# Columns 1024 to 1535 of gate_a on VectorE, ahead of the attention, through a ring of slab buffers

## The chip, the cores and the metric

The kernel runs on one core of a Trainium2 chip. The core has five engines that run beside each other, each through its own instructions in order: TensorE (PE in the profile, its weight loads PEld), VectorE (DVE), ScalarE (ACT), GpSimd (POOL) and SyncE (SP), which here only issues DMAs. They meet at semaphores. The metric is the time on the device in microseconds (us). Three runs of the kernel before took 1679.76, 1679.78 and 1680.25 us.

## The reference, cut to what matters

One layer: adaLN-modulated token mixing (eight mLSTM heads and a pooling mixer), then an MLP. There are 128 context tokens and 256 latent tokens, so 384 tokens in all; the context is modulated by `c_ctx`, the latents by `c`.

```python
def _adaln(cond, ada_w, ada_b):
    mod = jax.nn.silu(cond) @ ada_w + ada_b
    return mod.reshape(cond.shape[0], N_MOD, D_MODEL)      # 6 x 2048
...
    shift_a, scale_a, gate_a, shift_f, scale_f, gate_f = [mod[:, i][:, None, :] for i in range(N_MOD)]
    h = _rmsnorm(x, norm_w[0]) * (1 + scale_a) + shift_a
    proj = h @ w_in                                        # q, k, v, o, gates, u
...
    mix = jnp.concatenate([hm, hp], axis=-1) @ w_out
    x = x + gate_a * _rmsnorm(mix, norm_w[1])
    h = _rmsnorm(x, norm_w[2]) * (1 + scale_f) + shift_f
    y = jnp.square(jax.nn.relu(h @ w1)) @ w2
    x = x + gate_f * _rmsnorm(y, norm_w[3])
```

`ada_w` is 2048 x 12288 in float32, about 100 MB. The case is about the product of silu of the two condition vectors with a few of its columns: `gate_a`, modulation 2, which is first needed when the output projection `w_out` is done.

## The kernel before, in words

All large products run on TensorE as three passes each (high half by high, high by low, low by high, in a reduced float32 format), at lines 149 to 151. A weight slab of 128 x 1024 is brought in by SP (`load_w`, line 132, three raw buffers), ScalarE makes its high half (`hi`, line 138) and VectorE its low half (`lo`, line 139), four buffers each. A projection group is `gemm_T`: two accumulators of 128 x 384 and four such slabs, 24 matmuls for each. After each slab it calls its *feeds*: generators that put other work in between, so many steps for each slab as their rate says.

The stages around the change are: `u` and `v` (line 512) until about 197 us; `qk(0)`, the first group of q and k, which is eight slabs with the pooling mixer and the mLSTM gates as feeds, until about 247 us; `qk(1)` to `qk(3)`, 24 slabs with the attention of the heads before as feeds; the four groups of `o`, 16 slabs; and `w_out` (`wo`), 32 slabs, until about 610 us.

The modulation is done in two ways:

- **By TensorE** (`ada_gate`, line 239): slabs of 128 x 512 of `ada_w` are the moving operand of plain float32 matmuls with 32 columns of weights, four of them side by side in the array (a *set*). A part of 512 columns takes 16 such matmuls, four sets. Before the change, `mat` does `gate_a`'s columns 1024 to 1535 and 1536 to 2047 so, eight sets. Their slabs land in the memory of `masks` and in `gslab`. `ada_rows` then copies the sums out by ScalarE (line 277) and turns them by small matmuls (line 281).
- **By VectorE** (`ada_vec`): a slab holds two or one of the 16 rows of a partition; for each row and condition one instruction adds row times condition into the accumulator `ada_acc` (line 324 the first, `TENSOR_SCALAR`; line 326 the others, `SCALAR_TENSOR_TENSOR`). Then a set of matmuls with ones sums over the partitions (`adav`, line 339), ScalarE copies the sums out (`adav_sb`, line 341), and small matmuls turn them (`adaf`, line 345). `mid_vec` does five pieces of 1024 columns so: `scale_f`, `shift_f` and the first half of `gate_a`; as feed `ada2` it goes at 1.5 steps for each slab during `qk(1)` to `qk(3)`, then at 1.3. Its slabs are in four buffers of 512 KB of the pool `adap`. At three of its steps and at each end it moves `mat` on (`beside`).

The order within each engine is set by the Tile scheduler from the program's dependencies and its own priorities; it is fixed when the kernel is built.

Of the kernel before, what the change touches and what calls it, by code (L numbers as in the profile page):

```python
# [7 lines left out]
F32 = mybir.dt.float32  # L8
# [5 lines left out]
P = 128  # L14
# [14 lines left out]
N_ADA = 4  # L29
# [7 lines left out]
S_FIRST, S_LAST, N_LAST = 1, 6, 2  # L37
LAG = 4
N_AHEAD = 3
RATES = (1.5, 1.3, 1.3)  # L40
GATE_AT = 1, 6, 10


# [1 line left out]
def hymba_kernel(  # L45
# [6 lines left out]
    nc = tc.nc  # L52
# [6 lines left out]
    adap = ada_scope.enter_context(tc.tile_pool(name="adap", bufs=1, side="right"))  # L59
# [6 lines left out]
    def bank(name):  # L66
        return psum.tile([P, 512], F32, tag="ps", name=name)
# [11 lines left out]
    masks = vp.tile([P, N_CST - 3, P], F32, name="masks")  # L79
# [139 lines left out]
    aw = ada_w.rearrange("(p j) n -> p j n", j=16)  # L219
# [25 lines left out]
    def ada_mat(parts, tags=("ada",), raws=None):  # L245


        n, nk = len(parts), parts[0][2]
        w, nj = nk * P, 8 // nk
        ps = bank(f"ada_{parts[0][0]}_{parts[0][1]}")  # L250
        for b, (i, k0, _) in enumerate(parts):
            c0 = i * D + k0 * P
            for j0 in range(0, 16, nj):
                tag = tags[b % len(tags)]
                raw = raws.pop(0) if raws else None
                if raw is None:
                    raw = (wp if tag == "lo" else adap).tile([P, nj, w], F32, tag=tag, name=f"ada_raw_{i}_{k0}_{j0}", bufs=N_W if tag == "lo" else N_ADA)
                    nc.sync.dma_start(raw, aw[:, j0:j0 + nj, c0:c0 + w])
                for a in range(nj):
                    j = j0 + a  # L260
                    g = j % 4
                    nc.tensor.matmul(ps[32 * g:32 * g + 32, 0:w], cT[:, j, 6 - 2 * b:38 - 2 * b], raw[:, a, :],
                                     start=b == 0 and j < 4, stop=b == n - 1 and j >= 12)
                if b < n - 1 or j0 + nj < 16:
                    yield
        yield from ada_rows(parts, ps)
# [32 lines left out]
    vec = {}  # L299

    def ada_vec(i, c, n):


        acc = vec["acc"].tile([P, 2, n], F32, tag="adaacc", name=f"ada_acc_{i}_{c}", bufs=1)
        c0, nj = i * D + c, vec["slab"] // n

        def load(t):
            raw = vec["pool"].tile([P, nj, n], F32, tag="ada", name=f"ada_raw_{i}_{c}_{t}", bufs=vec["bufs"])
            nc.sync.dma_start(raw, aw[:, nj * t:nj * t + nj, c0:c0 + n])
            return raw  # L310

        beside = vec.get("beside", {})
        raw = load(0)
        yield
        for t in range(16 // nj):
            if t in beside:
                next(beside[t], None)
            more = t < 16 // nj - 1
            ahead = load(t + 1) if more and vec["bufs"] > 1 else None
            for a in range(nj):  # L320
                for g in range(2):
                    cj = sg[:, g, nj * t + a:nj * t + a + 1]
                    if t == 0 and a == 0:
                        nc.vector.tensor_scalar(acc[:, g, :], raw[:, a, :], cj, None, op0=ALU.mult)
                    else:
                        nc.vector.scalar_tensor_tensor(acc[:, g, :], raw[:, a, :], cj, acc[:, g, :], op0=ALU.mult, op1=ALU.add)  # L326
            raw = load(t + 1) if more and ahead is None else ahead
            if more:
                yield
        yield  # L330
        w = n // 2
        nk = w // P
        if "end" in beside:
            next(beside["end"], None)
        ps = bank(f"adav_{i}_{c}")
        for h in range(2):
            for g in range(2):
                r = 32 * (2 * h + g)
                nc.tensor.matmul(ps[r:r + 32, 0:w], ones[:, 0:32], acc[:, g, h * w:(h + 1) * w], start=True, stop=True)
        sb = vec["pool"].tile([P, 512], F32, tag="adasb", name=f"adav_sb_{i}_{c}", bufs=1)  # L340
        nc.scalar.activation(sb[:, 0:w], ps[:, 0:w], AF.Copy)
        yield
        pf = bank(f"adaf_{i}_{c}")
        for k in range(nk):
            nc.tensor.matmul(pf[:, 4 * k:4 + 4 * k], sb[:, k * P:(k + 1) * P], ident[:, 0:P:32], start=True, stop=True)
# [154 lines left out]
    for s in range(NS):  # L500
        for ci, (kind, c0, w) in enumerate(chunks):
            k0, nk = ksteps[s]
            load_ahead(5 * s + ci, 1 if s + ci == 0 else N_AHEAD)
            hi, lo, n = loaded.pop(5 * s + ci)
            acc = [bank(f"{kind}_{c0}_{s}_{i}") for i in range(3)]
# [295 lines left out]
        yield  # L801

    def mid_vec():
        for i, q in ((4, 0), (4, 1), (3, 0), (3, 1), (2, 0)):
            yield from ada_vec(i, 1024 * q, 1024)

    ada2 = Feed(mid_vec(), RATES[0])

    def qk(g, feeds):
        gemm_T(w_in, [g * 256], hx, NTOK, evac_q, feeds, name="q")  # L810
        gemm_T(w_in, [M + g * 256], hx, NTOK, evac_k, feeds, name="k")
# [6 lines left out]

    fxt = Feed(store_xT(), 3.0)
    fp_, fg_ = Feed(pooling(), 1.0), Feed(gates(), 1.0)  # L820
    qk(0, (fxt, fg_, fp_))
    fxt.finish()
    fg_.finish()
    fp_.finish()
# [1 line left out]
    att_scope = ExitStack()  # L826
    acc_scope = ExitStack()
    accp = acc_scope.enter_context(tc.tile_pool(name="accp", bufs=1, side="right", reuse_waits="tile"))
    vec.update(pool=adap, acc=accp, slab=1024, bufs=N_ADA)
    att = att_scope.enter_context(tc.tile_pool(name="att", bufs=2, reuse_waits="tile"))  # L830

    gslab = att.tile([P, 1, 512], F32, name="gslab", bufs=1)
    mat = ada_gate([(2, 8, 4), (2, 12, 4)], (masks.rearrange("p n q -> p (n q)").rearrange("p (j c) -> p j c", c=512), gslab))
    vec.update(beside={GATE_AT[0]: mat, GATE_AT[1]: mat, GATE_AT[2]: mat, "end": mat})
    fa = []
    for g in range(1, 4):
        fa.append(Feed(attention(g - 1), 1.0))
# [490 lines left out]
    def w1_group(g, feeds=(), n=NTOK):  # L1328
        gemm_T(w1, [grp(g)], hx2, n, evac_pair, feeds, name="w1")

    for ch in range(8):
        if ch < S_FIRST:
            w1_group(4, (ff, fx), 386)
            mlp_out(ch, (ff, fx, fn))
            fn.finish()
            for g in range(5, 8):
                w1_group(g, (ff,))
        elif ch <= S_LAST:
            if ch == S_FIRST:
                fx.finish()  # L1340
                while not vec.get("half"):
                    next(ff.gen)
                for scope in (xb_scope, acc_scope, ada_scope):
                    scope.close()
                str_scope = ExitStack()
                strp = str_scope.enter_context(tc.tile_pool(name="strp", bufs=1, side="right", reuse_waits="tile"))
                vec.update(pool=strp, acc=strp, slab=512, bufs=1, half=False)
                ff.rate = RATE_GS
                r16, r7 = strp.tile([P, 2, 2, 512], F32, name="r16"), strp.tile([P, 2, 512], F32, name="r7")
                for n in range(3):  # L1350
                    free += [wp.tile([P, 1024], F32, tag="raw", name=f"raw_a{n}", bufs=3), strp.tile([P, 1024], F32, name=f"raw_b{n}")]
# [79 lines left out]
```

## Time and profile before

| what | us |
|---|---|
| median of three runs | 1679.78 |
| the profiled execution | 1679.09 |
| its span, first to last instruction | 1677.4 |
| PE busy | 1648.3 |
| PEld busy | 1496.6 |
| DVE busy | 1328.4 |
| ACT busy | 751.1 |

The span is what the trace covers; the 1.7 us between it and the execution's time lie around it. Busy times of different engines overlap. TensorE's clock was granted in full (9 of tenths, the highest digit, in each of the 40 slices). In a timeline row the columns are the start, the length, engine, line, operation, output and inputs, shape and count; a bracket holds the idle time ahead and what ended it. In a windows row they are the stretch and its length, then the busy time of each engine with its instructions, granted clock, share of the DMA engines, and GB/s.

### The profile page before, as it was taken

Reading aid. Unit: us, or ns where it says so; the run is one execution under the profiler, and the core shown is the slowest. Engines: PE = TensorE matmul, PEld = TensorE weight load, DVE = VectorE, ACT = ScalarE, POOL = GpSimd, SP = SyncE. Lnnn points to the kernel's source line nnn. Section 1 sums busy time; section 2 is a strip of 40 time slices with the busy share of each in tenths; the row PEclk is TensorE's granted clock in tenths of the full one; section 3 lists DMA queues with packets and bytes.
Section 4 is the critical chain, followed back from the end, with each engine's and each line's share of the span. In section 5 each row is a group of like instructions: output and inputs, shape, how many; then the busy total and the mean of one; then the engine's idle time right before and its main releaser. Section 6 shows DMA issues by size and latency. Waiting matters only on the chain.

```text
span 1677.4 us, 24412 instructions
## 1 busy us (share of the span) xinstructions
PE 1648.3 (98%) x9249; PEld 1496.6 (89%) x9249; DVE 1328.4 (79%) x1971; ACT 751.1 (45%) x1224; POOL 133.1 (8%) x185
## 2 busy tenths in 40 slices
PE   6999999999999999999999999999999999999997
PEld 4888999999999989989988988988988988988986
DVE  3677669898999959997688787589788488488687
ACT  5322345555443345543444444444445354354452
POOL 1000002221000024530000000000000000000220
PEclk9999999999999999999999999999999999999999
DMA  9999757787789964754446445255544343443662
GB/s 328 329 309 304 246 175 247 239 250 229 239 262 309 319 202 137 213 153 126 136 150 203 125 133 177 87 169 162 153 151 136 116 151 116 136 125 112 197 193 103
DMA packets 231461, 320.72 MB, mean 191 GB/s; under 512 B 14784, under 2 KB 169872, under 8 KB 230960
## 3 DMA queue, kind: packets, MB, share of 16 engines
q1 hardware_dynamic: 223920, 303.42, 57.3%
q0 software_dynamic: 5984, 13.78, 2.9%
q10 hardware_dynamic: 1440, 1.97, 0.3%
q8 instruction: 72, 1.18, 0.3%
q14 instruction: 45, 0.37, 0.1%
HBM read 308.61 MB, written 10.51 MB: 190 GB/s over the span
## 4 chain that ended last, share of the span: by engine, by line
PE 78%; DVE 13%; DMA 5%; issue 3%; ACT 0%; POOL 0%; SPq 0%; DVEq 0%; ACTq 0%; POOLq 0%
PE acc_w L151 10%; PE acc_w L150 10%; PE acc_w L149 10%; PE v L512 4%; PE u L512 4%; PE y L1239 3%; PE y L1240 3%; PE y L1238 3%; DVE ada_acc L326 3%; DMA ada_raw<-in_ada_w_dram 2%; DVE lo_t L1224 2%; PE y L1082 2%; PE y L1083 2%; PE y L1081 2%; PE y_yz L1240 1%
## 5 line engine op out<-in xcount | busy, mean ns | idle before, releaser
L150 PE MATMUL acc_w<-h2l,hi_w 128*128 128x384 f32 (+1 forms) x1024 | 346.0, 338 | 0.5 <-DVE h2l L1033 0.5
L149 PE MATMUL acc_w<-h2h,hi_w 128*128 128x384 f32 (+1 forms) x1024 | 344.7, 338 | 1.2 <-ACT h2h L1029 1.2
L151 PE MATMUL acc_w<-h2h,lo_w 128*128 128x384 f32 (+1 forms) x1024 | 344.9, 337 | 0.6 <-DVE lo_w L139 0.6
L326 DVE SCALAR_TENSOR_TENSOR ada_acc<-ada_raw,sg,ada_acc 128x1024 f32<-128x1024 f32 (+1 forms) x240 | 252.8, 1081 | 32.1 <-DMA ada_raw<-in_ada_w_dram 32.1
L149 PEld LDWEIGHTS acc_w<-h2h,hi_w 128*128 128x128 f32 x1024 | 192.2, 188 | 4.0 <-ACT h2h L1029 2.0
L150 PEld LDWEIGHTS acc_w<-h2l,hi_w 128*128 128x128 f32 x1024 | 192.5, 188 | 1.8 <-DVE h2l L1033 0.8
L151 PEld LDWEIGHTS acc_w<-h2h,lo_w 128*128 128x128 f32 x1024 | 192.1, 188 | 2.2 <-DVE lo_w L139 1.9
L139 DVE TENSOR_TENSOR lo_w<-raw_b,hi_w 128x1024 fp32r<-128x1024 f32 x52 | 62.9, 1219 | 37.5 <-ACT hi_w L138 37.5
L139 DVE TENSOR_TENSOR lo_w<-raw_a,hi_w 128x1024 fp32r<-128x1024 f32 x52 | 63.1, 1219 | 35.7 <-ACT hi_w L138 35.6
L138 ACT ACTIVATE hi_w<-raw_b 128x1024 fp32r<-128x1024 f32 x52 | 54.9, 1057 | 62.7 <-PE acc_w L150 47.6
L138 ACT ACTIVATE hi_w<-raw_w 128x1024 fp32r<-128x1024 f32 x48 | 50.7, 1055 | 68.7 <-PE acc_w L150 36.5
L1223 ACT ACTIVATE hi_t<-raw_b 128x1024 fp32r<-128x1024 f32 x52 | 55.2, 1062 | 58.5 <-PE y L1240 28.3
L1223 ACT ACTIVATE hi_t<-raw_a 128x1024 fp32r<-128x1024 f32 x52 | 55.2, 1061 | 54.3 <-PE y L1240 26.5
L138 ACT ACTIVATE hi_w<-raw_a 128x1024 fp32r<-128x1024 f32 x52 | 54.8, 1057 | 53.6 <-PE acc_w L150 41.0
L139 DVE TENSOR_TENSOR lo_w<-raw_w,hi_w 128x1024 fp32r<-128x1024 f32 x48 | 58.4, 1218 | 22.0 <-ACT hi_w L138 21.9
L138 ACT ACTIVATE hi_wo<-raw_wo 128x1024 fp32r<-128x1024 f32 x32 | 33.9, 1063 | 80.1 <-DMA raw_wo<-in_w_out_dram 65.1
L1224 DVE TENSOR_TENSOR lo_b<-raw_b,hi_b 128x1024 fp32r<-128x1024 f32 x40 | 48.8, 1221 | 24.9 <-ACT hi_b L1223 24.6
L1223 ACT ACTIVATE hi_b<-raw_a 128x1024 fp32r<-128x1024 f32 x38 | 40.2, 1058 | 62.2 <-PE acc_w L150 46.2
L1223 ACT ACTIVATE hi_b<-raw_b 128x1024 fp32r<-128x1024 f32 x40 | 42.3, 1057 | 56.6 <-PE acc_w L150 45.3
L1224 DVE TENSOR_TENSOR lo_b<-raw_a,hi_b 128x1024 fp32r<-128x1024 f32 x38 | 46.2, 1221 | 22.4 <-ACT hi_b L1223 22.4
L1224 DVE TENSOR_TENSOR lo_t<-raw_a,hi_t 128x1024 fp32r<-128x1024 f32 x52 | 63.0, 1214 | 0.3 <-ACT hi_t L1223 0.2
L1224 DVE TENSOR_TENSOR lo_t<-raw_b,hi_t 128x1024 fp32r<-128x1024 f32 x52 | 62.9, 1215 | 0.0
(2286 smaller groups left out, 4243.7 us busy)
## 6 DMA issues: line engine op xcount, KB each, us to landing
ada_raw<-in_ada_w_dram SPq DMA_DIRECT2D x130, 512.0 KB, 5.2
raw_a<-in_w_dram SPq DMA_DIRECT2D x104, 512.0 KB, 4.1
raw_b<-in_w_dram SPq DMA_DIRECT2D x104, 512.0 KB, 4.2
raw_w<-in_w_dram SPq DMA_DIRECT2D x48, 512.0 KB, 4.2
raw_wo<-in_w_out_dram SPq DMA_DIRECT2D x32, 512.0 KB, 5.3
u<-in_ada_w_dram SPq DMA_DIRECT2D x18, 512.0 KB, 5.9
raw_u<-in_w_in_dram SPq DMA_DIRECT2D x16, 512.0 KB, 7.0
raw_q<-in_w_in_dram SPq DMA_DIRECT2D x16, 512.0 KB, 5.0
```

Source lines behind the costliest of these rows:

```text
L138: nc.scalar.activation(hi[:, 0:n], raw[:, 0:n], AF.Copy)
L139: low = lambda: nc.vector.tensor_tensor(lo[:, 0:n], raw[:, 0:n], hi[:, 0:n].bitcast(F32), op=ALU.subtract)
L149: nc.tensor.matmul(ps, lh, rh, start=start, stop=False)
L150: nc.tensor.matmul(ps, lh, rl, start=False, stop=False)
L151: mm3.ins = nc.tensor.matmul(ps, ll, rh, start=False, stop=stop).ins
L326: nc.vector.scalar_tensor_tensor(acc[:, g, :], raw[:, a, :], cj, acc[:, g, :], op0=ALU.mult, op1=ALU.add)
L512: nc.tensor.matmul(acc[i][:, 0:n], h[k0 + k][a][:, i * P:(i + 1) * P], (hi, lo)[b][:, k, :], start=k == 0 and a + b == 0, stop=k == nk - 1 ...
L1223: nc.scalar.activation(hi, raw, AF.Copy)
L1224: nc.vector.tensor_tensor(lo, raw, hi.bitcast(F32), op=ALU.subtract)
L1238: nc.tensor.matmul(banks[m], xh, wh, start=start and h + j == 0, stop=False)
L1239: nc.tensor.matmul(banks[m], xh, wl, start=False, stop=False)
L1240: nc.tensor.matmul(banks[m], xl, wh, start=False, stop=stop and h + j == 2)
```

## The change

Columns 1024 to 1535 of `gate_a` leave `mat` and become a first piece of `mid_vec`, 512 columns wide, with two rows in a slab. The feed `ada2` now also runs in `qk(0)`, at one step for each slab; from `qk(1)` on its rate is 1.6 instead of 1.5. The four slab buffers are now taken once, as `ring`: three hold slabs in turn, and the fourth is the accumulator of the first piece and joins the ring once its sums are taken. `mat` has one part, so four sets instead of eight, and 512 KB DMAs into the ring take the place of half of those into `masks` and `gslab`.

```diff
-RATES = (1.5, 1.3, 1.3)
+RATES = (1.6, 1.3, 1.3)
+RATE_V = 1.0
@@ ada_mat @@
+                mine = raw is None and tag == "ada" and vec.get("ring")
+                if mine:
+                    buf = mine.pop(0)
+                    raw = buf.rearrange("p (j c) -> p j c", j=nj)
+                    nc.sync.dma_start(raw, aw[:, j0:j0 + nj, c0:c0 + w])
...
+                if mine:
+                    mine.append(buf)
@@ ada_vec @@
-        acc = vec["acc"].tile([P, 2, n], F32, tag="adaacc", name=f"ada_acc_{i}_{c}", bufs=1)
+        ring, own = vec.get("ring"), vec.get("own")
+        if own is None:
+            acc = vec["acc"].tile([P, 2, n], F32, tag="adaacc", name=f"ada_acc_{i}_{c}", bufs=1)
+        else:
+            acc, vec["own"] = own.rearrange("p (g n) -> p g n", g=2), None
...
-            raw = vec["pool"].tile([P, nj, n], F32, tag="ada", name=f"ada_raw_{i}_{c}_{t}", bufs=vec["bufs"])
+            raw = (vec["pool"].tile([P, nj, n], F32, tag="ada", name=f"ada_raw_{i}_{c}_{t}", bufs=vec["bufs"]) if ring is None
+                   else ring.pop(0).rearrange("p (j c) -> p j c", j=nj))
...
+            if ring is not None:
+                ring.append(raw.rearrange("p j c -> p (j c)"))
...
+        if own is not None:
+            ring.append(own)
@@ mid_vec and its callers @@
     def mid_vec():
+        yield from ada_vec(2, 1024, 512)
+        vec.update(mid)
         for i, q in ((4, 0), (4, 1), (3, 0), (3, 1), (2, 0)):
             yield from ada_vec(i, 1024 * q, 1024)
-    ada2 = Feed(mid_vec(), RATES[0])
+    ring = [adap.tile([P, 1024], F32, tag="ada", name=f"ring{i}", bufs=N_ADA) for i in range(N_ADA)]
+    vec.update(pool=adap, slab=1024, bufs=N_ADA, ring=ring, own=ring.pop())
+    mid = {}
+    ada2 = Feed(mid_vec(), RATE_V)
...
-    qk(0, (fxt, fg_, fp_))
+    qk(0, (fxt, fg_, fp_, ada2))
...
-    vec.update(pool=adap, acc=accp, slab=1024, bufs=N_ADA)
+    vec.update(acc=accp)
+    ada2.rate = RATES[0]
...
-    mat = ada_gate([(2, 8, 4), (2, 12, 4)], (masks.rearrange("p n q -> p (n q)").rearrange("p (j c) -> p j c", c=512), gslab))
-    vec.update(beside={GATE_AT[0]: mat, GATE_AT[1]: mat, GATE_AT[2]: mat, "end": mat})
+    mat = ada_gate([(2, 12, 4)], (masks.rearrange("p n q -> p (n q)").rearrange("p (j c) -> p j c", c=512), gslab))
+    mid.update(beside={GATE_AT[0]: mat, GATE_AT[1]: mat, GATE_AT[2]: mat, "end": mat})
```

Every instruction of the five pieces that follow is placed anew with it. In the rows below, lines of the changed kernel are up to 17 higher than those before (326 is 339 now, 339 is 354, 341 is 358, 345 is 362). On VectorE, in `qk(0)` before the change, around the low halves of k's second and third slab and of the pooling mixer's third group (`p20l`, `p21l`; `lo_pw3` is from a pooling weight; `acol` to `glast` are the gates' last copies):

```order
L645 COPY acol_2056<-ps_col_2329 128x3x8 x2
L645 COPY ecol_2057<-ps_col_2335 128x24 x2
L645 COPY gcol_2058<-ps_col_2341 128x2x8 x2
L649 COPY nT_2060<-ps_n0_2346 128x16
L650 COPY glast_2059<-ps_n0_2346 128x40
L139 TENSOR_TENSOR lo_k_1024_1_2433<-raw_k_1024_1_2430,hi_k_1024_1_2432 128x1024
L139 TENSOR_TENSOR lo_k_1024_2_2482<-raw_k_1024_2_2479,hi_k_1024_2_2481 128x1024
L139 TENSOR_TENSOR lo_pw3_2528<-raw_pw3_2525,hi_pw3_2527 128x512
L200 TENSOR_TENSOR p20l_2413<-pool_2_0_2408,p20h_2412 128x384
L200 TENSOR_TENSOR p21l_2421<-pool_2_1_2416,p21h_2420 128x384
```

and with it (`ring0` to `ring2` are slabs, `ring3` is the accumulator):

```order
L667 COPY glast_2059<-ps_n0_2361 128x40
L140 TENSOR_TENSOR lo_k_1024_1_2458<-raw_k_1024_1_2455,hi_k_1024_1_2457 128x1024
L339 SCALAR_TENSOR_TENSOR ring3_2069<-ring2_2068,sg_111,ring3_2069 128x512 x2
L140 TENSOR_TENSOR lo_k_1024_2_2512<-raw_k_1024_2_2509,hi_k_1024_2_2511 128x1024
L339 SCALAR_TENSOR_TENSOR ring3_2069<-ring2_2068,sg_111,ring3_2069 128x512 x2
L339 SCALAR_TENSOR_TENSOR ring3_2069<-ring0_2066,sg_111,ring3_2069 128x512 x2
L140 TENSOR_TENSOR lo_pw3_2558<-raw_pw3_2555,hi_pw3_2557 128x512
L201 TENSOR_TENSOR p20l_2433<-pool_2_0_2428,p20h_2432 128x384
L201 TENSOR_TENSOR p21l_2441<-pool_2_1_2436,p21h_2440 128x384
L339 SCALAR_TENSOR_TENSOR ring3_2069<-ring0_2066,sg_111,ring3_2069 128x512 x2
L339 SCALAR_TENSOR_TENSOR ring3_2069<-ring1_2067,sg_111,ring3_2069 128x512 x4
```

Of the 32 new instructions, 26 now stand ahead of `p20l_2433`, six behind `p21l_2441`, and none behind k's last low half.

On TensorE, at the end of the first piece of 1024 columns (`adav_0`, `adaf_0`; `num` and `inter` are the attention's), in `qk(2)`'s k, before the change:

```order
L749 MATMUL inter_1_0_3410<-C_1_0_3136,q_2855 128x129
L749 MATMUL inter_1_0_3410<-C_1_2_1_3325,q_2855 128x129
L742 MATMUL num_1_1_3424<-v_84,e_3135 128x129 x2
L749 MATMUL inter_1_1_3427<-C_1_0_3136,q_2857 128x129
L749 MATMUL inter_1_1_3427<-C_1_2_1_3325,q_2857 128x129
L345 MATMUL adaf_0_3444<-cst,adav_sb_0_3368 128x4 x4
L149 MATMUL acc_k_0_3374<-hh_739,hi_k_1_3455 128x384
```

There `adav_0` stands 31 rows ahead of `adaf_0`, behind the set of `ada_gate` that precedes k's first slab: a whole slab and the attention's eight matmuls lie between the two. With the change:

```order
L766 MATMUL inter_2_1_3526<-C_1_1_0_3355,q_2900 128x129
L766 MATMUL inter_2_1_3526<-C_1_1_3174,q_2900 128x129
L240 MATMUL ada_gate<-masks,cT 32x512 x3
L240 MATMUL ada_gate<-gslab,cT 32x512
L354 MATMUL adav_0_3547<-ada_acc_0_2805,cst 32x512 x4
L150 MATMUL acc_k_0_3403<-hh_1187,hi_k_2_3565 128x384
L151 MATMUL acc_k_0_3403<-hl_1188,hi_k_2_3565 128x384
L152 MATMUL acc_k_0_3403<-hh_1187,lo_k_2_3566 128x384
L150 MATMUL acc_k_1_3404<-hh_1187,hi_k_2_3565 128x384
L151 MATMUL acc_k_1_3404<-hl_1188,hi_k_2_3565 128x384
L362 MATMUL adaf_0_3554<-cst,adav_sb_0_3552 128x4 x4
L152 MATMUL acc_k_1_3404<-hh_1187,lo_k_2_3566 128x384
```

The set and `adav_0` have moved to the next slab but one, and five matmuls of `acc_k` are left between `adav_0` and `adaf_0`. At two other ends of pieces it is alike: six matmuls between the pair `adav_1024` and `adaf_1024` of the second piece (24 slab matmuls and more before), and four at the end of the last piece (24 before). The new first piece has nine between its pair.

On ScalarE, around the copy `adav_sb_0` that stands between the two, before the change:

```order
L138 ACTIVATE hi_k_3_3566<-raw_k_3_3564 128x1024
L755 ACTIVATE dn_0_0_3336<-num_0_0_3332 128x2
L755 ACTIVATE dn_0_1_3347<-num_0_1_3343 128x2
L758 ACTIVATE hs_0_3331<-num_0_0_3332,dn_0_0_3336 128x128
L758 ACTIVATE hs_0_3331<-num_0_1_3343,dn_0_1_3347 128x128
L341 ACTIVATE adav_sb_0_3368<-adav_0_3363 128x512
L760 ACTIVATE sq_0_3335,ssh<-hs_0_3331 128x128
L760 ACTIVATE sq_1_3346,ssh<-hs_0_3331 128x128
L138 ACTIVATE hi_q_0_3610<-raw_q_0_3608 128x1024
```

and with it:

```order
L139 ACTIVATE hi_q_1_3723<-raw_q_1_3721 128x1024
L768 ACTIVATE nsb_2_0_3510<-inter_2_0_3509,gcol 128x129 x2
L768 ACTIVATE nsb_2_1_3527<-inter_2_1_3526,gcol 128x129 x2
L772 ACTIVATE dn_2_0_3516<-nsb_2_0_3510 128x2
L772 ACTIVATE dn_2_1_3533<-nsb_2_1_3527 128x2
L775 ACTIVATE hs_2_3505<-nsb_2_0_3510,dn_2_0_3516 128x128
L775 ACTIVATE hs_2_3505<-nsb_2_1_3527,dn_2_1_3533 128x128
L358 ACTIVATE adav_sb_0_3552<-adav_0_3547 128x512
L777 ACTIVATE nsb_2_0_3510,ssh<-hs_2_3505 128x128
L777 ACTIVATE nsb_2_1_3527,ssh<-hs_2_3505 128x128
```

The copy has moved from behind `hs_0`, the first outputs' scaling, to behind both scalings of `hs_2`, the third outputs' (each waits for `dn_2`, which VectorE makes from `nsb_2`, and that from `inter_2`).

More of the change, by code (lines that the diff above doesn't have):

```diff
@@ L255, in ada_mat @@
                 raw = raws.pop(0) if raws else None
-                if raw is None:
+                mine = raw is None and tag == "ada" and vec.get("ring")
[3 more added lines that the diff above has]
+                    nc.sync.dma_start(raw, aw[:, j0:j0 + nj, c0:c0 + w])
+                elif raw is None:
                     raw = (wp if tag == "lo" else adap).tile([P, nj, w], F32, tag=tag, name=f"ada_raw_{i}_{k0}_{j0}", bufs=N_W if tag == "lo" else N_ADA)
@@ L917, in hymba_kernel @@
     vec.pop("beside")
+    mid.clear()
     def token_rstd_rows(accs, name, between=None):
@@ L1346, in hymba_kernel @@
                 strp = str_scope.enter_context(tc.tile_pool(name="strp", bufs=1, side="right", reuse_waits="tile"))
-                vec.update(pool=strp, acc=strp, slab=512, bufs=1, half=False)
+                vec.update(pool=strp, acc=strp, slab=512, bufs=1, half=False, ring=None)
                 ff.rate = RATE_GS
```

## The prediction

> **What bounds the kernel now.** I read the page's busy times first, then its shares of the chain that ended last, then the windows of the stages which the change touches, then single rows of TensorE's timeline there.
>
> ```profile
> span 1677.4 us, 24412 instructions
> PE 1648.3 (98%) x9249; PEld 1496.6 (89%) x9249; DVE 1328.4 (79%) x1971; ACT 751.1 (45%) x1224; POOL 133.1 (8%) x185
> ...
> PE 78%; DVE 13%; DMA 5%; issue 3%; ACT 0%; POOL 0%; SPq 0%; DVEq 0%; ACTq 0%; POOLq 0%
> ...
> core 0: us, PE busy (x) PEld busy (x) DVE busy (x) ACT busy (x) POOL busy (x), PEclk, DMA share, GB/s
> 184.50:229.40 44.90, 44.90 (x298) 43.22 (x296) 28.89 (x64) 20.54 (x32) 1.07 (x2) 1.00 0.65 199
> 184.50:241.00 56.50, 56.50 (x367) 54.82 (x366) 32.52 (x68) 25.27 (x39) 1.07 (x2) 1.00 0.61 185
> 411.00:527.00 116.00, 116.00 (x689) 112.02 (x687) 109.39 (x135) 47.15 (x90) 4.00 (x4) 1.00 0.78 252
> 480.00:500.00 20.00, 20.00 (x117) 18.92 (x116) 20.00 (x19) 6.43 (x9) 0.00 (x0) 1.00 0.82 260
> ```
>
> TensorE is busy 98% of the span and in all of the first two windows, so what it need not do there comes off the time, as long as nothing else holds it up. The first two windows are where the new VectorE work goes: of 56.5 us VectorE has 24.0 free. The third is the second half of o and the first half of w_out: VectorE is at 109.39 of 116, and full for 20 us of it. There it is nearly as tight as TensorE.
>
> **What TensorE is spared.** A set of `ada_gate` between slab matmuls, and one ahead of an `adav`:
>
> ```profile
> 428.51 0.34 PE L151 MATMUL acc_o<-hh,lo_o 128*128 128x384 f32 x1
> 428.78 0.63 PE L239 MATMUL ada_gate<-masks,cT 128*32 128x512 f32 x3
> ...
> 430.06 0.34 PE L150 MATMUL acc_o<-hl,hi_o 128*128 128x384 f32 x1
> 430.23 0.34 PE L151 MATMUL acc_o<-hh,lo_o 128*128 128x384 f32 x1
> ...
> 388.12 0.63 PE L239 MATMUL ada_gate<-masks,cT 128*32 128x512 f32 x3
> ...
> 389.00 1.04 PE L339 MATMUL adav<-ada_acc,cst 128*32 128x512 f32 x8
> ```
>
> Slab matmuls start 0.17 to 0.18 us apart (430.06 to 430.23). Without the set, the second one behind 428.51 would start at 428.86; it starts at 430.06, so a set between them costs 1.20 us, the slower first matmul behind it included. Ahead of `adav` a set costs 389.00 - 388.12 = 0.88. Before, four sets of each kind make 8.32. With the change two of each kind are left, 4.16. **Spared: 4.16 us.**
>
> **What TensorE gets.** The new piece's `adav`, 256 columns wide, and two small `adaf`:
>
> ```profile
> 793.14 0.33 PE L151 MATMUL acc_w<-h2h,lo_w 128*128 128x384 f32 x1
> 793.40 0.64 PE L339 MATMUL adav<-ada_acc,cst 128*32 128x256 f32 x8
> 793.97 0.44 PE L149 MATMUL acc_w<-h2h,hi_w 128*128 128x384 f32 x1
> 794.25 0.33 PE L150 MATMUL acc_w<-h2l,hi_w 128*128 128x384 f32 x1
> ...
> 1430.52 0.33 PE L151 MATMUL acc_w<-h2h,lo_w 128*128 128x384 f32 x1
> 1430.69 0.50 PE L345 MATMUL adaf<-cst,adav_sb 128*128 128x4 f32 x4
> 1431.05 0.42 PE L149 MATMUL acc_w<-h2h,hi_w 128*128 128x384 f32 x1
> 1431.31 0.34 PE L150 MATMUL acc_w<-h2l,hi_w 128*128 128x384 f32 x1
> ```
>
> By the same count: 794.25 - 793.14 - 0.35 = 0.76, and 1431.31 - 1430.52 - 0.35 = 0.44. **Added: 1.20 us.** The small matmuls behind `ada_gate` stay four, only with narrower output. TensorE's own account is -4.16 + 1.20 = -2.96 us.
>
> **VectorE in qk(0).** 32 instructions of 512 columns: two `TENSOR_SCALAR` and 30 `SCALAR_TENSOR_TENSOR`. The trace has both, in gate_f's pieces:
>
> ```profile
> L326 DVE SCALAR_TENSOR_TENSOR ada_acc<-ada_raw,sg,ada_acc 128x512 f32<-128x512 f32 x90 | 64.6, 745 | 32.1 <-DMA ada_raw<-in_ada_w_dram 32.1
> L324 DVE TENSOR_SCALAR ada_acc<-ada_raw,sg 128x512 f32<-128x512 f32 x6 | 2.9, 477 | 2.7 <-PE adav L339 2.7
> ```
>
> 2 x 0.477 + 30 x 0.745 = 23.3 us, against 24.0 free: it fits, but without room. What it may hold up are low halves behind it in VectorE's order; the tightest are the pooling's:
>
> ```profile
> 229.47 0.56 DVE L200 TENSOR_TENSOR p20l<-pool,p20h 128x384 fp32r<-128x384 f32 x1
> ...
> 233.80 0.34 PE L150 MATMUL poolo<-p20l,hi_pw 128*128 128x384 f32 x1
> ```
>
> 26 of the 32 stand ahead of `p20l`: 2 x 0.477 + 24 x 0.745 = 18.8 us, of which the 16.0 free until 229.4 (44.90 - 28.89) take all but 2.8. So `p20l` ends at about 232.8, where TensorE wants it at 233.80. One us is left; I take 0.1 for small waits, between 0 and 2 (all idle time before 229.4 would have to be of use, which the gates' own chain may prevent). SP's order changes too: slab loads into the ring wait for VectorE to be done with a buffer, and weight slabs stand behind them in SP's queue. In qk(0) that delays weights for k's last slab and the next q by up to the same 3 us. For k's last slab they lie ready 5.7 us before use:
>
> ```profile
> 234.74 1.23 DVE L139 TENSOR_TENSOR lo_k<-raw_k,hi_k 128x1024 fp32r<-128x1024 f32 x1 [4.04 <-ACT hi_k L138]
> ...
> 241.63 0.34 PE L151 MATMUL acc_k<-hh,lo_k 128*128 128x384 f32 x1
> ```
>
> The low half ends at 235.97 and is used at 241.63, so I take nothing. The eight DMAs more meet a share of 0.61; as many bytes are gone from 0.78 later.
>
> **The waits that are new.** TensorE now comes to an `adaf` a few matmuls behind its `adav`, and everything queued behind on TensorE waits for ScalarE's copy. For `adaf_0` of the first large piece the copy stands behind the scaling of the third outputs, as the rows of the order show. Before the change those ran like this:
>
> ```profile
> 328.80 0.61 PE L749 MATMUL inter<-C,q 128*128 128x129 f32 x4
> ...
> 329.90 1.27 DVE L326 SCALAR_TENSOR_TENSOR ada_acc<-ada_raw,sg,ada_acc 128x1024 f32<-128x1024 f32 x1
> ...
> 332.57 1.28 DVE L326 SCALAR_TENSOR_TENSOR ada_acc<-ada_raw,sg,ada_acc 128x1024 f32<-128x1024 f32 x1
> ...
> 333.49 1.06 ACT L138 ACTIVATE hi_q<-raw_q 128x1024 fp32r<-128x1024 f32 x1 [0.45 <-PE acc_k L150]
> 334.75 0.39 ACT L758 ACTIVATE hs<-nsb,dn 128x128 f32<-128x128 f32 x1
> ...
> 594.79 1.07 PE L339 MATMUL adav<-ada_acc,cst 128*32 128x512 f32 x8
> 595.92 0.60 ACT L341 ACTIVATE adav_sb<-adav 128x512 f32<-128x512 f32 x1
> ```
>
> From the start of the last `inter` the second `hs` took 6.34 us (328.80 to 335.14). TensorE wants `adaf_0` at about 3.4 us by the same clock: the `inter` group 0.5, the set 0.88, `adav` 1.0, five matmuls 1.0. The copy takes 0.60. If the chain ran as before, the wait would be 6.34 + 0.60 - 3.4 = 3.5 us. But the two `ada_acc` instructions and the `hi_q` that stood in it are no longer there in the new order. The first held the chain for some 0.4 (it ended at 331.17, the copy that feeds its successor some 0.4 sooner), the second for most of its 1.28, the `hi_q` for up to its 1.06. With all of them off it would be 0.5 to 0.8. **I take 1.2**, nearer the short end as they are gone from the order, with 0.5 and 3.5 as ends. For the other pairs, copy and `adav` alone need 596.52 - 594.79 = 1.73 us, and TensorE wants the `adaf` 1.8 us after `adav` with four matmuls between, later with six or nine: 0.3 us for the three together, up to 1.
>
> **The tight stage.** Around the middle of w_out:
>
> ```profile
> 521.93 1.22 DVE L139 TENSOR_TENSOR lo_wo<-raw_wo,hi_wo 128x1024 fp32r<-128x1024 f32 x1
> ...
> 523.27 0.38 PE L151 MATMUL acc_wo<-mx12h,lo_wo 128*128 128x384 f32 x1
> ...
> 534.01 1.06 PE L345 MATMUL adaf<-cst,adav_sb 128*128 128x4 f32 x8 [0.42 <-ACT adav_sb L341]
> ...
> 547.61 0.95 PE L281 MATMUL ada_gate<-cst,gsb 128*128 128x4 f32 x8
> ```
>
> The low half is done at 523.15 and used at 523.27. By then seven of the eight old sets are past (4 x 0.88 + 3 x 1.20 = 7.12) against the four new ones (4.16), the added 1.20, and `ada_gate`'s last small matmuls, which now stand ahead of this point (0.95): TensorE comes 0.8 us sooner, less 1.5 for the new waits, so 0.7 later than before. VectorE's work up to there, counted by the order, is half a us more, and the slab loads' turns move. The two nearly cancel; I take 0.5 of waiting, from 0 to 2, and give back 0.2 of the 0.42 at 534.01, which a copy behind a late weight made.
>
> **Sum:** -2.96 + 0.1 + 1.2 + 0.3 + 0.5 - 0.2 = -1.06, say **-1.1 us**. The profiled execution took 1679.09 (span 1677.4 and 1.7 around it), so 1678.0; the median of the runs lies 0.69 above it, so I forecast **1678.7**. A measurement of this kernel can tell about 0.2%, 3.4 us, from no change: this is within.
>
> **Rivals.**
>
> 1. *Nothing is given back.* The copies are in time, and the 0.42 goes: -2.96 - 0.42 = -3.4, so 1676.4, on the very border of 0.2%. For it: waits on ScalarE are 0% of the chain. Against: four pairs with little between.
> 2. *VectorE paces the middle.* The sets that go are half of these:
>
> ```profile
> L239 PE MATMUL ada_gate<-masks,cT x48: 592/604/617, 281.9 to 527.7; 128*32 128x512 f32 x48
> ```
>
>    They stood between 428.78 and 527.7, where VectorE is at 94% (109.39 of 116), with 0.1 us to spare at 523. If its order sets the pace, TensorE's spared time returns as waiting there: -1.1 becomes 0, so 1679.8. For it: 13% of the chain is VectorE, and VectorE is busy for all of 480 to 500 (20.00 of 20). Against: TensorE waited there for 0.42 us in all, and over the whole middle its 116.00 stand against 109.39. [...]
> 3. *The copies are late; slower.* Place: `adaf_0` behind the third outputs. At the 3.5 us of the old chain, with 1.0 for the other pairs: -2.96 + 3.5 + 1.0 = +1.5, so 1681.3. It decides from waits of 3.0 us on.
> 4. *The work is not hidden in qk(0).* VectorE comes later than I count, and pooling and k wait: 2 us beside the forecast's other terms, 1680.7; it would be more if the weights behind the ring loads were late as well.
>
> **How the numbers follow.** Forecast (1677.5 to 1680) 0.42; nothing given back 0.18; VectorE paces 0.17; copies late 0.15; not hidden 0.08. Half of the first rival is faster by over 0.2%: 0.09. Slower by over 0.2% (above 1683.1) takes both of the last two, or one at more than its price: 0.09. The rest, 0.82, is within. The range reaches from just below the first rival to just above the third: 1676.2 to 1682.0.
>
> **What would show it.** Four sets of `ada_gate` left, each at 0.88 or 1.20; no wait of TensorE from 190 to 247; a wait of about 1 us ahead of `adaf_0` in qk(2) put down to `adav_sb`; TensorE at 527 about 1 us sooner. Wrong would make me a wait of several us at any of these, a `lo_wo` late by more than 2 us in the middle, or a weight slab that SP holds back behind the ring.

## The result, and the profile after

The changed kernel takes 1691.87 us (median of six runs, 1687.67 to 1697.67), against 1680.01 beside it: 1.0078 of the time before, 95% interval 1.0067 to 1.009. It is slower by some 12 us. The prediction, 1678.7 with a range up to 1682.0, was wrong, and had given a chance of 0.09 to slower by over 0.2%.

The profiled execution took 1692.45 us, 13.36 more than the one before. The page's busy times and shares of the chain:

```profile
span 1690.7 us, 24412 instructions
PE 1649.8 (98%) x9229; PEld 1498.2 (89%) x9229; DVE 1347.9 (80%) x2005; ACT 751.4 (44%) x1225; POOL 132.7 (8%) x185
...
PE 73%; DVE 15%; issue 5%; DMA 5%; ACT 1%; POOL 1%; SPq 0%; DVEq 0%; POOLq 0%; ACTq 0%
```

VectorE has 19.5 us more to do. TensorE is busy 1.5 us more although four sets are gone; its share of the chain fell from 78% to 73%, VectorE's rose from 13% to 15%. The windows: qk(0), the attention stage from the end of the second q to the first o (before in the second fence), the middle:

```profile
core 0: us, PE busy (x) PEld busy (x) DVE busy (x) ACT busy (x) POOL busy (x), PEclk, DMA share, GB/s
184.50:241.00 56.50, 56.50 (x364) 54.54 (x363) 52.20 (x100) 24.94 (x39) 1.07 (x2) 1.00 0.81 257
267.00:416.00 149.00, 143.04 (x902) 135.70 (x901) 131.38 (x225) 75.33 (x210) 29.20 (x27) 0.99 0.72 228
411.00:527.00 116.00, 115.19 (x690) 113.64 (x689) 110.31 (x145) 49.61 (x96) 6.43 (x6) 1.00 0.79 252
```

```profile
267.00:405.00 138.00, 138.00 (x891) 132.21 (x890) 125.83 (x221) 74.89 (x207) 28.98 (x27) 1.00 0.78 247
```

qk(0) took the new piece with TensorE at 56.50 of 56.50. The attention stage grew most, from 138 to 149 us, with 6 us in which TensorE had nothing and 5.6 us more of VectorE's work. These are TensorE's rows with the large new waits (start, length, engine, line, operation, and in the bracket the idle time ahead and what ended it), in order of time:

```profile
333.79 1.05 PE L362 MATMUL adaf<-cst,adav_sb 128*128 128x4 f32 x8 [1.14 <-ACT adav_sb L358]
...
374.15 0.79 PE L766 MATMUL inter<-C,q 128*128 128x129 f32 x4 [2.00 <-DVE hs L776]
...
375.06 0.52 PE L151 MATMUL acc_k<-hl,hi_k 128*128 128x384 f32 x1
375.38 0.52 PE L152 MATMUL acc_k<-hh,lo_k 128*128 128x384 f32 x1
...
392.01 0.45 PE L152 MATMUL acc_o<-hh,lo_o 128*128 128x384 f32 x1 [0.85 <-DVE lo_o L140]
398.42 0.45 PE L704 MATMUL mb<-mrow,pick 104*128 104x384 f32 x1 [1.10 <-ACT hnT L817]
425.47 0.71 PE L766 MATMUL inter<-C,q 128*128 128x129 f32 x4 [0.81 <-DVE hs L776]
534.02 0.44 PE L152 MATMUL acc_wo<-mx12h,lo_wo 128*128 128x384 f32 x1 [1.04 <-DVE lo_wo L140]
607.37 1.06 PE L354 MATMUL adav<-ada_acc,cst 128*32 128x512 f32 x8
...
612.47 1.05 PE L362 MATMUL adaf<-cst,adav_sb 128*128 128x4 f32 x8 [3.13 <-ACT adav_sb L358]
613.38 0.49 PE L151 MATMUL acc_wo<-mx0l,hi_wo 128*128 128x384 f32 x1
613.66 0.52 PE L152 MATMUL acc_wo<-mx0h,lo_wo 128*128 128x384 f32 x1
613.99 0.52 PE L150 MATMUL acc_wo<-mx1h,hi_wo 128*128 128x384 f32 x1
```

The seven waits make 10.07 us. Behind two of them, from 375.06 and from 613.66, slab matmuls start 0.32 us apart instead of 0.175: nine and ten of them, 1.30 and 1.46 us. With TensorE's account at -2.96, 16.3 us have to be found for +13.36; these rows hold 12.8 of them, and four smaller waits (0.24, 0.27, 0.36 and, in the MLP, 0.82) 1.7; the 0.42 of before went, so some 2.2 us are in none of these rows. By the MLP's first matmuls (616.79 before, 630.10 after) the loss is complete, 13.31 us. Two kinds of wait stand out: copies of `adav_sb` that come late (4.27 us), and VectorE's results that come late (4.70).

Why the last copy was late is in ScalarE's rows, those after in the first fence, those before in the second, and in SP's rows after, in the third:

```profile
603.91 1.06 ACT L139 ACTIVATE hi_w<-raw_w 128x1024 fp32r<-128x1024 f32 x1 [2.49 <-DMA raw_w<-in_w_dram]
610.87 1.06 ACT L139 ACTIVATE hi_w<-raw_w 128x1024 fp32r<-128x1024 f32 x1 [5.90 <-DMA raw_w<-in_w_dram]
611.84 0.58 ACT L358 ACTIVATE adav_sb<-adav 128x512 f32<-128x512 f32 x1
```

```profile
594.72 1.06 ACT L138 ACTIVATE hi_w<-raw_w 128x1024 fp32r<-128x1024 f32 x1 [1.96 <-PE acc_wo L150]
595.92 0.60 ACT L341 ACTIVATE adav_sb<-adav 128x512 f32<-128x512 f32 x1
600.12 1.06 ACT L138 ACTIVATE hi_w<-raw_w 128x1024 fp32r<-128x1024 f32 x1 [3.60 <-PE acc_wo L150]
```

```profile
597.66 0.37 SPq L322 DMA_DIRECT2D ring<-in_ada_w_dram  x1
598.80 14.78 SPq L133 DMA_DIRECT2D raw_w<-in_w_dram  x5
```

`hi_w` is the first weights of the MLP, not needed for some time. Before the change one of them stood ahead of the copy, and its data was there. Now two do, and ScalarE sat 5.90 us idle for the second one's data; the copy, whose sums had been ready since 608.4, stood behind it, and TensorE behind the copy. SP had issued the last ring load only at 597.66, one slab later in the program than before, with the weights behind it. It issued the second `hi_w`'s weights at 600.84, and they took 10 us to land, where a `raw_w` took 4.2 in the median of the whole run. From 598 to 611 the DMA engines' share was 1.01, but at that place before the change, from 590 to 603, it was 1.01 too. How much of the lateness is the ring's was not tried.

### The profile page after: what moved, and what is told of

Its sections match the earlier page's. It is cut to its first block, busy times and chain, and to the rows that moved or that the text cites. A ratio compares the mean times of both kernels' runs of the same rounds, so it can differ in the third digit from the quotient of the medians.

```text
span 1690.7 us, 24412 instructions
## 1 busy us (share of the span) xinstructions
PE 1649.8 (98%) x9229; PEld 1498.2 (89%) x9229; DVE 1347.9 (80%) x2005; ACT 751.4 (44%) x1225; POOL 132.7 (8%) x185
## 4 chain that ended last, share of the span: by engine, by line
PE 73%; DVE 15%; issue 5%; DMA 5%; ACT 1%; POOL 1%; SPq 0%; DVEq 0%; POOLq 0%; ACTq 0%
PE acc_w L150 9%; PE acc_w L152 9%; PE acc_w L151 9%; PE v L529 4%; PE u L529 4%; PE y L1263 3%; PE y L1264 3%; PE y L1262 3%; DVE ada_acc L339 3%; DVE lo_t L1248 2%; PE acc_wo L150 2%; PE acc_wo L152 2%; PE acc_wo L151 2%; PE y L1106 2%; PE y L1107 2%
## 5 line engine op out<-in xcount | busy, mean ns | idle before, releaser
L339 DVE SCALAR_TENSOR_TENSOR ada_acc<-ring,sg,ada_acc 128x1024 f32<-128x1024 f32 (+1 forms) x180 | 208.6, 1190 | 0.9 <-DMA ring<-in_ada_w_dram 0.9
L339 DVE SCALAR_TENSOR_TENSOR ada_acc<-ada_raw,sg,ada_acc 128x512 f32<-128x512 f32 x60 | 43.3, 746 | 32.6 <-DMA ada_raw<-in_ada_w_dram 32.6
```

## The experiments

Three theories: **P**, TensorE waits for ScalarE's copy at the pieces' ends; **D**, VectorE is too full in the attention stage, so chains and low halves are late; **R**, the ring's loads hold up SP and the weights everywhere. By a step of a feed: with 1.6 steps a slab and three steps of the new piece in qk(1), `adav` and `adaf` now fall into the same slab at four of six pieces; before they did at none. Each kernel was timed against the kernel before in the same session; a ratio is to that. How much less a kernel takes than the changed one is a difference of medians from different sessions: the kernel before had 1679.09 to 1680.17 in them, and the changed kernel's own runs lie 10 us apart. A microsecond or two of such a difference means little.

**e1: `adaf` one slab later.** For the pieces with both in one slab, on the changed kernel (in short):

```diff
-        pf = bank(f"adaf_{i}_{c}")
-        ...
+        def adaf(): ...
+        if len(steps_done) == slab:
+            late.append(adaf)      # issued when the next slab's feeds begin
+        else:
+            adaf()
```

> The changed kernel, but an adaf that would fall into the same slab as its adav (four of the six pieces) is issued one slab later; nothing else of the order moves on TensorE. Theory P (TensorE waits for ScalarE's copy because adav and adaf now share a slab): the waits of 1.14 and 3.13 us ahead of adaf go, and with the second one the slow stretch behind it (about 1.6 us): 5.9 us, so about 1686. Theory D (VectorE's order in the attention stage is denser, its chains and low halves are late): the other waits, some 7.5 us, stay, so not below 1685. Theory R (the ring's loads hold up SP and with it the weights): the low half or the copy is late all the same, 1690 or more.

1685.62 us, ratio 1.0034 (1.0021 to 1.0047): 6.3 us less than the changed kernel, as P said. Of the copies' 4.27 us, one wait of 1.43 was left; the waits on VectorE stayed in sum, partly at other places (one of 2.26 on `lo_o` at 391).

**e2: the old slabs.** The new piece faster, the rest as before the change:

```diff
-RATES = (1.6, 1.3, 1.3)
-RATE_V = 1.0
+RATES = (1.5, 1.3, 1.3)
+RATE_V = 1.4
...
-    ada2.rate = RATES[0]
+    ada2.rate, ada2.due = RATES[0], 0.0
```

> The changed kernel with the new piece at 1.4 steps a slab instead of 1.0, so that its 11 steps end within qk(0), and the rate behind it back at 1.5 from a clean start: every later piece has the slabs that it had before the change; the two sets of ada_gate that go, the ring and the new piece stay. Theories P and D (what costs is in which slabs the pieces' steps fall): the waits of the changed kernel go and TensorE's account of -2.96 is left, with something for a tighter qk(0): 1677 to 1680. Theory R: the ring is still there, 1686 or more.

1682.42 us, ratio 1.0015 (1.0006 to 1.0024). Four fifths of the loss are gone with ring, new piece and sets all in place, so theory R as the main cause falls. It isn't the gain that P and D left room for: 2.3 us slower than before. Its profile shows 0.42 for the tighter qk(0) and 1.14 at the new piece's own `adaf`.

**e3: only the rate back.** `RATES = (1.5, 1.3, 1.3)` on the changed kernel.

> The changed kernel with 1.5 steps a slab in the attention stage instead of 1.6; all pieces end one to two slabs later and other pairs of adav and adaf share a slab (the first two-slab pieces (2,1024) and (4,1), and (2,0) no longer). Theory D: the attention waits of about 5.7 us go for the most part, 1684 to 1687. Theory P: the two adaf waits that were seen are at pieces that no longer share a slab, so 4.3 and 1.6 go, 1686; a new one may come at (4,1). Theory R: 1690 or more.

1689.62 us, ratio 1.0054 (1.0042 to 1.0067). The times of P and D missed, and R's bound, 1690, fits best; but in e2 the ring was there without this cost, and in e4, next, the cost without the ring. And D's waits did go: from the attention stage to the MLP one on VectorE is left, 0.80 us. What took their place are two waits for a copy, 1.75 and 2.50 us, and slow matmuls behind both. The second came 24 matmuls, a whole slab, behind its `adav`, so nearness isn't the whole of P:

```profile
604.95 1.06 PE L354 MATMUL adav<-ada_acc,cst 128*32 128x512 f32 x8
612.90 1.44 PE L362 MATMUL adaf<-cst,adav_sb 128*128 128x4 f32 x6 [2.50 <-ACT adav_sb L358]
```

**e4: only the new rate, on the kernel before.** `RATES = (1.6, 1.3, 1.3)`, no ring, no new piece, eight sets.

> The kernel before with 1.6 steps a slab in the attention stage instead of 1.5, nothing else: no ring, no new piece, all eight sets. Pieces (4,0), (4,1) and (3,1) have adav and adaf in one slab. Theories P and D: slower than before although none of the change is in it, by 3 to 9 us, 1683 to 1689. Theory R: 1680.

1689.85 us, ratio 1.0055 (1.0041 to 1.0068): 9.7 us slower, with nothing of what the change is about. TensorE's rows show waits of the same two kinds:

```profile
319.84 1.06 PE L345 MATMUL adaf<-cst,adav_sb 128*128 128x4 f32 x8 [2.26 <-ACT adav_sb L341]
...
373.96 0.71 PE L749 MATMUL inter<-C,q 128*128 128x129 f32 x4 [1.36 <-DVE hs L759]
...
392.93 1.41 PE L345 MATMUL adaf<-cst,adav_sb 128*128 128x4 f32 x6 [2.00 <-ACT adav_sb L341]
```

**e5: e2 with e1's edit.**

> e2 (later pieces in their old slabs) with e1's edit as well: the new piece's adaf comes one slab behind its adav. In e2 TensorE waited 1.14 us there. Theory P: that goes, so e2's 1682.4 becomes about 1681. If the placing of steps is all that the change costs, TensorE's account of -2.96 should then stand nearly free, 1677 to 1678.

1681.9 us, ratio 1.0015 (1.0006 to 1.0023), the same as e2. The 1.14 went, and its profile had waits on VectorE of 0.92 and 0.80 in the attention stage instead. With the later pieces' steps where they were, the change still costs 2.4 us.

**e6: e3 with e1's edit.**

> e3 (1.5 steps a slab, pieces in yet other slabs) with e1's edit: no adaf in the slab of its adav. e3's profile showed waits of 1.75 and 2.50 us ahead of two adaf, each followed by a stretch at about half pace (1.5 and some 4 us). Theory P: these go, about 9 us, so 1680 to 1682. Were it VectorE's order (theory D) that costs in e3, it would stay near 1688.

1693.38 us, ratio 1.0081 (1.0068 to 1.0095). A plain miss, and on the wrong side of e3 by 4 us. At 620 TensorE waited 3.40 us for the same copy as in e3; at 474 to 480 it waited 3.96 us around an `adav` and its `adaf`, the `adav` for VectorE's last sums. Moving `adaf` a slab away is no cure in itself.

**e7: the sets alone.** The kernel before with `mat = ada_gate([(2, 12, 4)], ...)` and the missing columns copied from the next 512.

> The kernel before without the ada_gate work of gate_a's columns 1024 to 1535: these columns are left out of the computation and filled with a copy of the next 512 columns' result. Four sets of TensorE's go, nothing is added, no step moves. TensorE's account: -4.16, so 1675.8. If VectorE paces the middle (rival 2 of the prediction), the time stays at 1680.

1678.56 us, ratio 0.9995 (0.9987 to 1.0004): a gain of 1.0 us, not 4.2, and within what can't be told from none. The profile tells where the rest went. At the end of `w_out` (ScalarE's squares of the last outputs, before first, then e7) TensorE is 3.23 us ahead:

```profile
609.08 1.02 ACT L898 ACTIVATE sq_mo<-acc_wo 128x384 f32<-128x384 f32 x2 [2.81 <-PE acc_wo L151]
```

```profile
605.85 1.02 ACT L900 ACTIVATE sq_mo<-acc_wo 128x384 f32<-128x384 f32 x2 [2.78 <-PE acc_wo L151]
```

In the MLP, 280 us later and far from the change, it returns as one wait and slow matmuls behind it, again before first:

```profile
890.04 0.50 PE L1239 MATMUL y_yz<-lo_b,hid13h 128*128 128x512 f32 x1 [0.20 <-DVE lo_b L1224]
```

```profile
889.35 0.51 PE L1241 MATMUL y_yz<-lo_b,hid13h 128*128 128x512 f32 x1 [2.13 <-DVE lo_b L1226]
...
890.41 0.63 PE L1241 MATMUL y_yz<-lo_b,hid15h 128*128 128x512 f32 x1
890.83 0.63 PE L1242 MATMUL y_yz<-hi_b,hid15l 128*128 128x512 f32 x1
```

In both, VectorE's chain to `lo_b` had waited for the DMA of `raw_a`, before first:

```profile
887.62 1.23 DVE L1271 TENSOR_TENSOR raw_b<-raw_a,raw_b 128x1024 f32<-128x1024 f32 x1 [0.93 <-DMA raw_a<-in_w_dram]
```

```profile
886.94 1.23 DVE L1273 TENSOR_TENSOR raw_b<-raw_a,raw_b 128x1024 f32<-128x1024 f32 x1 [1.89 <-DMA raw_a<-in_w_dram]
```

Just ahead of the wait TensorE was 2.62 us ahead, the data 0.7. Behind it seven matmuls start 0.43 us apart instead of 0.23 (granted clock 0.61 from 889 to 893), some 1.6 us more. With that the lead is gone: at 903.5 e7 is 0.13 behind. That is one profile; the wait was not tried by itself, and in the profiles of the other kernels it is between none and 1.06 us.

**e8: the piece alone.** e2 with `mat` back at both parts.

> e2 with all eight sets of ada_gate: columns 1024 to 1535 are computed twice, by VectorE in qk(0) and by TensorE as before. Only the addition is priced: 1.20 us of adav and adaf, the wait of 1.14 at its adaf, some 0.4 in qk(0): 1682.8. By e2 less the four sets it would be 1682.4 + 4.2 = 1686.6; which of the two it is tells whether the four sets are worth 4.16 us here.

1685.32 us, ratio 1.0035 (1.0022 to 1.0049), between the two. By the ratios the four sets are worth 0.20% here, 3.4 us, where e7 gave 1.0; the intervals are wide enough for both to be true. The addition costs more than the 2.7 us counted, and where the rest is was not found: the profiled execution (1681.3 of span) is the shortest of its runs.

**e9: one copy moved.** On the changed kernel, the last piece's copy ahead of the MLP's weights in ScalarE's order:

```diff
-        nc.scalar.activation(sb[:, 0:w], ps[:, 0:w], AF.Copy)
+        cp = nc.scalar.activation(sb[:, 0:w], ps[:, 0:w], AF.Copy).ins
+        if (i, c) == (2, 0):
+            copies.append(cp)
...
-            for ins in after:
+            for ins in (*after, *(copies if name.startswith("w1") else ())):
                 es.enter_context(tc.issue_after(ins))
```

> The changed kernel with one copy moved in ScalarE's order: adav_sb of the last piece (2,0) now stands ahead of the two hi_w of the next stage's weights, not behind them; TensorE's order is the same word for word. Its profile had a wait of 3.13 us for this copy, followed by ten matmuls at half pace (1.46 us). Theory P, made narrower (the copy is late because it queues behind a hi_w whose weights come late by DMA): both go for the most part, 4 to 4.6 us, so 1687 to 1688. If the copy is late for another reason, 1692.

1686.05 us, ratio 1.0037 (1.0025 to 1.005): 5.8 us less, from one instruction of 0.6 us. ScalarE's rows and TensorE's:

```profile
606.66 0.60 ACT L359 ACTIVATE adav_sb<-adav 128x512 f32<-128x512 f32 x1 [6.51 <-PE adav L355]
607.16 1.05 ACT L140 ACTIVATE hi_w<-raw_w 128x1024 fp32r<-128x1024 f32 x1
```

```profile
607.16 0.34 PE L151 MATMUL acc_wo<-mx0h,hi_wo 128*128 128x384 f32 x1
607.33 1.04 PE L365 MATMUL adaf<-cst,adav_sb 128*128 128x4 f32 x8
```

The same `adaf`, four matmuls behind the same `adav`, has no wait at all. It was the place in the queue.

**e10: e3 with e9's edit.**

> e3 with the same single move. There adav and adaf of piece (2,0) stand 30 matmuls and a slab apart, and TensorE waited 2.50 us all the same, followed by the end of w_out at half pace (about 4 us). Theory P, narrower: 6 us less than e3's 1689.6, so 1683 to 1684. If nearness of adav and adaf were the cause, this changes nothing, 1689 to 1690.

1685.79 us, ratio 1.0036 (1.0022 to 1.005): 3.8 us less than e3, where 6 were expected. The wait of 2.50 is gone; a smaller one (1.48, on ScalarE's squares) and a slow stretch behind it came in its place. Nearness would have changed nothing.

**e11: less on VectorE.** The changed kernel without 30 of the 64 sums of the two `scale_f` pieces (those of the second condition, but for the first row):

```diff
-                for g in range(2):
+                for g in range(1 if t and i == 4 else 2):
```

> The changed kernel with less on VectorE in the attention stage and nothing moved on TensorE: pieces (4,0) and (4,1) leave out the sum of the second batch row but for its first term (30 of 64 instructions of 1.19 us); loads, steps and slabs are the same. Theory D (the chains of the attention and the low halves queue behind the pieces' instructions on a full VectorE): the waits on VectorE of the changed kernel from 313 to 426 us (2.00 with 1.3 of half pace behind it, 0.85, 0.81, 0.36, 0.27, 0.24) go, about 6 us, so 1686, more if the copy waits there shrink too. If they come from late loads instead, 1690 to 1692.

1686.36 us, ratio 1.0039 (1.0027 to 1.0052): 5.5 us less, as D said. By ScalarE's reads of the accumulators the first o ends 4.0 us behind the kernel before, instead of 10.7. The chain that held TensorE at 374.15 in the changed kernel, in VectorE's rows, and the same in e11:

```profile
371.10 0.22 DVE L773 TENSOR_TENSOR dn<-dn,ecol 128x2 f32<-128x2 f32 x2
371.24 1.28 DVE L339 SCALAR_TENSOR_TENSOR ada_acc<-ring,sg,ada_acc 128x1024 f32<-128x1024 f32 x1
372.44 0.22 DVE L774 RECIPROCAL dn<-dn 128x2 f32<-128x2 f32 x2
372.58 1.26 DVE L339 SCALAR_TENSOR_TENSOR ada_acc<-ring,sg,ada_acc 128x1024 f32<-128x1024 f32 x1
373.76 0.60 DVE L776 SCALAR_TENSOR_TENSOR hs<-num,dn,hs 128x128 f32<-128x128 f32 x2
```

```profile
369.50 0.22 DVE L773 TENSOR_TENSOR dn<-dn,ecol 128x2 f32<-128x2 f32 x2
...
369.71 0.22 DVE L774 RECIPROCAL dn<-dn 128x2 f32<-128x2 f32 x2
369.84 1.26 DVE L339 SCALAR_TENSOR_TENSOR ada_acc<-ring,sg,ada_acc 128x1024 f32<-128x1024 f32 x1
371.03 0.60 DVE L776 SCALAR_TENSOR_TENSOR hs<-num,dn,hs 128x128 f32<-128x128 f32 x2
```

From `dn` to `hs` 2.66 us with two `ada_acc` in between, 1.53 with one; TensorE's wait there is 1.06 instead of 2.00. The edit takes off more than the change put on: VectorE is busy 1314.8 us, against 1347.9 with the change and 1328.4 before. With less on VectorE the ring's buffers may also come free sooner; whether that has a part in it isn't told apart here.

**e12: e9 and e11 together.**

> e9 and e11 in one kernel: the last piece's copy ahead of the two hi_w, and 30 of VectorE's instructions of pieces (4,0) and (4,1) left out. e9 took 5.8 us off the changed kernel, e11 5.5. If the two causes are separate and together nearly all of what the change costs, 1680 to 1681.5; if they share a part, 1683 or more.

1679.29 us, ratio 1.0 (0.9991 to 1.0009): 12.6 us less than the changed kernel, all of what the change had cost. The two causes are separate and nearly add up (5.8 and 5.5 alone). The profiles, one for each kernel, show it by place. The table has how far each kernel is behind the kernel before, in us, at ScalarE's squares ahead of `w_out`'s end (590.18 before) and at the MLP's first matmuls (616.79 before):

| kernel | at the squares | at the MLP's start |
|---|---|---|
| changed | 8.36 | 13.31 |
| e3, rate back | 1.78 | 9.02 |
| e9, copy moved | 6.52 | 6.61 |
| e11, less on VectorE | 2.09 | 9.13 |
| e12, e9 and e11 | 0.25 | 0.33 |

Less on VectorE, or the old rate, takes away most of the first loss; moving the copy takes away the second. e9's edit moves an instruction behind the first place only, so the 1.84 us between it and the changed kernel there are a measure of the spread from one profile to the next. None of the twelve is faster than the kernel before and computes everything.

## Why the prediction was wrong, point by point

- **qk(0).** Right. The rows after: `p20l` ends at 231.93 (forecast 232.8), TensorE takes it at 234.22 without a wait, and its rows from 184 to 262 have none.

```profile
231.38 0.55 DVE L201 TENSOR_TENSOR p20l<-pool,p20h 128x384 fp32r<-128x384 f32 x1
```

```profile
234.22 0.34 PE L151 MATMUL poolo<-p20l,hi_pw 128*128 128x384 f32 x1
```

- **TensorE's account.** The sets went as forecast: 24 and 8 matmuls of `ada_gate` are left of 48 and 16. Taken off alone they bring 3.23 us by the end of their stages and 1.0 by the end of the kernel (e7). The prediction took time spared in a stage as time off the end; a wait on a DMA in the MLP, with 0.20 us showing before, and slow matmuls behind it took it back in that profile.
- **The first large piece's `adaf`.** Right in place and size: 1.14 us against 1.2, and for the reason given. From the last `inter` to the second `hs` the chain took 4.13 us, where the forecast implies 4.0.
- **The other pairs: the step that failed first.** "For the other pairs, copy and `adav` alone need 596.52 - 594.79 = 1.73 us ... 0.3 us for the three together, up to 1." The last one took 3.13, and 1.46 of slow matmuls. I counted the copy's length and the matmuls ahead of `adaf`, and not what stands ahead of the copy on ScalarE. The order rows of the two kernels would have told it, one `hi_w` ahead before and two now, and the stall of 0.42 at 534.01 was named in the prediction as a copy behind a late weight; the lesson of it was applied to that row alone. e9 settles this: 5.8 us for that place by the medians; in the profiles 4.95 us are lost between the squares and the MLP's start, and 0.09 in e9.
- **The rate: the step that is missing.** No term of the sum is about the 1.6 steps a slab from qk(1) to qk(3). The prediction worked out VectorE in qk(0) and in the middle, and not between, where it was busy for 125.83 of 138 us before; 5.6 us more went there. The old rate takes 6.6 us off the loss up to the squares (e3), though it then puts the last copy where it costs 7.2 us instead of 4.95. e11 shows that the means is VectorE, but it lightens VectorE below what it was before, so its 5.5 us are no measure of the rate. e4 shows that this one constant, with the pieces' ends it moves, costs 9.7 us on its own.
- **The tight stage.** 0.5 us forecast, 1.04 on `lo_wo` at 534.02; the 0.42 went as hoped. Too small to matter.
- **The rivals.** The third (late copies) was the right mechanism for one of the two losses, priced at the wrong piece: it would have ended at 1681.3. The second had VectorE as the bound in the middle; it became one, but in the attention stage. SP holding weights back was listed as what would make the prediction wrong, and worked out in qk(0) only. Late weights are part of what happened at the end of `w_out`; whether SP's order or the full DMA engines made them late is open.
- **What stays open.** With all steps in their old slabs (e2, e5) the change costs 2.3 us, 5 more than TensorE's account. At `w_out`'s last squares (609.08 before) e2's profile is 0.19 us ahead and e5's 1.38 behind, so the rest of their lag, 1.4 and 1.5 us, comes from the MLP. What makes it there is not shown.

## What to carry to other kernels

When a change moves steps in a fixed order, read for each wait what stands ahead of the awaited instruction on its own engine, and what that one waits for: a copy of 0.6 us behind a weight split that needs a late DMA cost 5.8 us. A constant that is changed along with the main idea is a change of its own and wants a term and a run of its own; here it cost 9.7 us by itself (e4), and taking it back alone returned only 2.3 (e3), because it also sets where the pieces end. And time spared on the busiest engine can be lost at the next wait that doesn't depend on it, as in e7's profile; so look for near-waits (0.20 us on a DMA) further down the program.

## What the runs showed of the hardware

A wait on TensorE cost more than itself at two places of the changed kernel: 1.30 us more behind the wait of 2.00, and 1.46 behind that of 3.13. The windows, one behind the first wait and one around the second:

```profile
374.50:378.00 3.50, 3.50 (x15) 3.50 (x14) 3.09 (x6) 2.98 (x11) 1.44 (x2) 0.52 0.80 276
612.00:618.00 6.00, 5.53 (x26) 5.54 (x27) 1.63 (x5) 0.41 (x1) 0.00 (x0) 0.72 0.69 240
```

The granted clock (the third number from the end) is 0.52 in the first and 0.72 in the second, against 0.996 over the whole span. In the two stretches nine and ten slab matmuls start 0.32 us apart instead of 0.175. Other kernels had such stretches behind waits of 1.75 and 2.50 us (e3; 1.5 and some 4 us lost) and of 3.67 (e11, again 0.32 us apart), and around three waits of 3.96 us together (e6: six matmuls of `adav` took 1.93 us, where eight take 1.06 in the changed kernel). At the end of `w_out` twelve small matmuls (`tr_r`) took 2.72 us behind a wait of 1.48 (e10), against 1.48 in the changed kernel. In the MLP seven matmuls of 512 columns started 0.43 us apart instead of 0.23 behind 2.13 us (e7). Behind waits of 2.26 and 2.51 on `lo_o` (e1 at 391, e9 at 390) there was none: the next six matmuls and more start 0.17 to 0.18 us apart. Nor was there one behind the single waits of 1.14 (e2), 1.36 (e4 at 374) and, in the changed kernel, 1.14, 1.10 and 1.04 us. So the length of the wait alone doesn't decide; what else does was not shown.
